# More sets of gathered expert rows multiplied beside the dense half of a PEER layer

## The chip, the core and the metric

The kernel runs on one core of a Trainium2 chip. Five engines work from queues of their own, each in order: TensorE (PE in the profile, PEld its weight loads), VectorE (DVE), ScalarE (ACT), GpSimd (POOL) and SyncE (SP). Data comes by DMA, issued from the queues of SP, ACT and POOL; indirect gathers are issued from POOL. TensorE writes to PSUM, which has eight banks of 128 x 512 floats. The metric is the device time of one execution in microseconds.

## What is computed

One layer of a diffusion backbone on 256 latent tokens and 256 context tokens, width 2048: a modulated norm, an input projection, a bidirectional mLSTM and differential attention, their merge, an output projection, and then the part that matters here, a PEER retrieval over 16384 single-neuron experts, and a final norm. The PEER part in the reference:

```python
def peer(h, w_pq, sub_keys, expert_u, expert_v):
    q = (h @ w_pq).reshape(B, T, P_HEADS, 2, P_KEY_DIM // 2)          # 8 heads
    s = jnp.einsum('bthpd,hpnd->bthpn', q, sub_keys)                  # 2 x 128 keys
    s1, i1 = lax.top_k(s[..., 0, :], P_TOPK)                          # 16 of each
    s2, i2 = lax.top_k(s[..., 1, :], P_TOPK)
    cand_s = (s1[..., :, None] + s2[..., None, :]).reshape(...)
    cand_i = (i1[..., :, None] * N_KEYS + i2[..., None, :]).reshape(...)
    top_s, pos = lax.top_k(cand_s, P_TOPK)
    idx = jnp.take_along_axis(cand_i, pos, axis=-1)
    g = jax.nn.softmax(top_s, axis=-1)
    def block(args):                                                  # 128 tokens
        act = jax.nn.gelu(jnp.einsum('td,ted->te', hx, expert_u[ix]))
        return jnp.einsum('te,ted->td', gx * act, expert_v[ix])
```

Each token uses 8 x 16 experts: it needs the dot product of its vector with the expert's row of `expert_u`, a gelu, the gate, and the sum of the experts' rows of `expert_v` with these weights.

## The kernel before

Matrices are split into a part rounded to TensorE's fast float form ("hi") and the rest ("lo"): ACT casts, DVE (in one of four cases POOL) subtracts (`stage`, lines 126 to 137), and three products are summed.

**U.** All 16384 rows of `expert_u` are multiplied with all tokens, whether they are used or not. The experts form 128 columns of 128. `u_pair` (1219) takes two columns: for each, 32 products, 16 with "hi" against both parts of the tokens (128x512) and 16 with "lo" (128x256), into one bank of the pool `psS`, which has four. The loop at 1631 then reduces the bank with DVE (1640), applies the gelu on ACT (1641) and writes the activations to a table in DRAM, `ag_dram`, from ACT's queue (1645). `made[0]` counts the columns so far.

Beside U, in small steps, runs a generator, `plan` (1463): after every half column `pump(pace[0])` (253) takes some steps of it, `pace[0]` of them on average (1.7 while the lists are made, then 1.25 and at last 1.3). It does the two top-16 searches (`retrieve`), writes the gates into the same DRAM table (`gate_map`, `map_out`), and makes lists of the used experts (`lists`, 1299). When 126 columns are through, `drain()` (1633) runs what is left of it at once.

**Blocks.** The 256 tokens are two tiles of 128, each of four groups of 32. A used expert goes into a block of 128 experts of one kind. Kinds 0 to 3 hold experts that only one group of tile 0 uses, kinds 4 to 7 the same for tile 1, six blocks each (`CAPS`, 57); other kinds are for experts of one tile, of one group in each tile, and of any tokens. `fill` (1347) gives places in the order of the columns: the first five blocks of each group from the columns under `EARLY` = 104, the sixth from all 126 (loop at 1391). The last two columns are taken whole. Four blocks, one of each group of a tile, are a set: `SETS[t][i]`.

**V.** For a block, POOL gathers 128 rows of `expert_v`, 8 KB each (`stage_rows`, 1507), and the experts' activations and gates from `ag_dram` (`stage_gates`, 1519; for the first five blocks only from the columns under `EARLY`). DVE multiplies these into weights (`weights_of`, 1542). In a set each block fills only 32 of TensorE's columns, and `v_groups` (1592) issues the four groups side by side, 16 products (32 instructions in the trace) for the 2048 output columns. The sum of a tile stays in four PSUM banks, `out_acc[t]`. Those of tile 0 are there as soon as `psG`, two banks of the lists, is released at the start of `soon` (1600); those of tile 1 take the place of `psS` when U is over (1654).

`soon` is the last part of `plan`. It gathers the rows of the first two sets, waits until `EARLY` columns are made, and then takes set after set: gates and rows of one set while the set before is multiplied. Its list is `SOON`, five sets of tile 0, which are multiplied beside U, and the first two of `ITEMS`, which are only gathered. After U the rest of `ITEMS` follows: two whole columns, a mixture of sets, paired, shared and single blocks, and at the end three sets. Before the last two sets the sum of tile 0 is closed, and its residual, norm and output run beside them.

**What sets the order.** Products go to TensorE, gathers to POOL and U's loads to SP in program order (`keep_in_program_order`). Everything else is placed by a planner in the build that simulates a timeline. Rows lie in a ring: four buffers of two rows until U is over, six after that (`two_rows`, 1494).

Of the kernel before, what the change touches and what calls it, by code (L numbers as in the profile page):

```python
# [19 lines left out]
F32 = mybir.dt.float32  # L20
# [6 lines left out]
OP = mybir.AluOpType  # L27
AX = mybir.AxisListType
PSUM = bass.MemoryType.PSUM
DRAM = bass.MemoryType.DRAM  # L30

P = 128
D = 2048
T = 256
# [18 lines left out]


N_LIST = P - 2
EARLY = 104
CAPS = (6,) * 8 + (8, 8, 16) + (1,) * 16
BASE = tuple(sum(CAPS[:i]) for i in range(len(CAPS)))
BOTH, PAIR, DENSE = 10, 11, 27
TILES = [(g // 4,) for g in range(8)] + [(0,), (1,)] + [(0, 1)] * 17  # L60
# [12 lines left out]
def spread(*groups):  # L73
    return [x for _, _, x in sorted(((i + 0.5) / len(g), j, x) for j, g in enumerate(groups) for i, x in enumerate(g))]
# [2 lines left out]


SETS = [[[(4 * t + j, i) for j in range(4)] for i in range(6)] for t in range(2)]
SOON = SETS[0][:5]  # L80
PAIRS = [[(PAIR + 4 * d + g, 0) for g in range(4)] for d in range(4)]
ITEMS = SETS[1][:2] + [[(DENSE, i)] for i in range(N_LIST, P)] + spread(
    SETS[1][2:4], PAIRS, [[(BOTH, i)] for i in range(CAPS[BOTH])], [[(8 + n % 2, n // 2)] for n in range(16)]) + [
    SETS[0][5], SETS[1][4], SETS[1][5]]


def build(tc, a, dump=None):
    nc = tc.nc
# [3 lines left out]
    def mp_(*args, **kw):  # L92
        tc.keep_in_program_order(mm(*args, **kw))  # L93
# [147 lines left out]
    side = []  # L241
# [920 lines left out]
    psM.release()  # L1162
    psA.release()

    psS = tc.alloc_tile_pool(name="psS", bufs=4, space=PSUM, side="right", reuse_waits="tile")
    psG = tc.alloc_tile_pool(name="psG", bufs=2, space=PSUM, reuse_waits="tile")


# [50 lines left out]
    def u_pair(i1, pace):  # L1219
        pss = []  # L1220
        for e in range(2):
            ps = psS.tile([P, 2, T], F32, name="s", tag="s")
            flat = ps.rearrange("p s t -> p (s t)")
            for hf_ in range(2):
                hl = take()
                for kk in range(8):
                    k = hf_ * 8 + kk
                    mp_(flat, lhsT=hl[0][:, kk * P:(kk + 1) * P], rhs=h2hl[k], start=k == 0, stop=False,
                        skip_group_check=True)
                for kk in range(8):  # L1230
                    k = hf_ * 8 + kk
                    mp_(ps[:, 1], lhsT=hl[1][:, kk * P:(kk + 1) * P], rhs=h2[0][k], start=False, stop=k == 15,
                        skip_group_check=True)
                pump(pace[0])
            pss.append(ps)
        return pss
# [62 lines left out]
    def lists():  # L1299
# [88 lines left out]
            nc.vector.tensor_tensor(k3[:, 0], k3[:, 0], gone, op=OP.subtract)  # L1388
        for t in range(2):
            four = single[:, 4 * t:4 * t + 4]  # L1390
            for first, n, w in ((0, CAPS[0] - 1, EARLY), (CAPS[0] - 1, 1, N_LIST)):
                yield from fill(four[:, :, 0:w], n, [BASE[4 * t + c] + first for c in range(4)])
                nc.vector.tensor_tensor(k2[:, t, 0:w], k2[:, t, 0:w], gone[:, 0:w], op=OP.subtract)
                if not first:
                    nc.vector.tensor_tensor(four[:, :, 0:w], four[:, :, 0:w], put[:, :, 0:w], op=OP.subtract)
        nc.vector.tensor_tensor(k3[:, 0], k3[:, 0], k2[:, 0], op=OP.add)
        nc.vector.tensor_tensor(k3[:, 0], k3[:, 0], k2[:, 1], op=OP.add)
# [109 lines left out]
    def stage_rows(kind, i):  # L1507
        raw = one_row()
        if kind == DENSE:
            nc.sync.dma_start(raw, FULL[i * P:(i + 1) * P, :])  # L1510
        else:
            gather(raw, FULL, idxV, BASE[kind] + i)
        return raw

    def gather(out, src, idx, b):
        tc.keep_in_program_order(nc.gpsimd.indirect_dma_start(  # L1516
            out=out, out_offset=None, in_=src, in_offset=bass.IndirectOffsetOnAxis(ap=idx[:, b:b + 1], axis=0)))

    def stage_gates(kind, i):
        if kind == DENSE:  # L1520
            return i
        n = len(TILES[kind])
        ag = gates.tile([P, 4 * P], F32, name="ag", tag="ag", bufs=12)[:, 0:2 * n * P]
        src = (ag_tile, ag_dram)[n - 1]
        gather(ag, src[0:2 * P * (1 + EARLY)] if kind < 8 and i < CAPS[kind] - 1 else src, idxG, BASE[kind] + i)
        return {t: ag[:, 2 * j * P:2 * (j + 1) * P] for j, t in enumerate(TILES[kind])}

    def split(raw):
# [13 lines left out]
    def weights_of(kind, ins):  # L1542
        if kind == DENSE:
            r = halves(act_tail[:, ins - N_LIST, :], T, "d", 2)
            return {t: [x[:, t * P:(t + 1) * P] for x in r] for t in range(2)}
        out = {}
        for t, ag in ins.items():
            if kind < 8 or kind >= PAIR:
                g = slice(32 * group(kind, t), 32 * group(kind, t) + 32)
                out[t] = vst.tile([P, 32], F32, name="w32", tag="w32", bufs=16)  # L1550
                nc.vector.tensor_tensor(out[t], ag[:, g], ag[:, P:][:, g], op=OP.mult)  # L1551
                continue
            w = vst.tile([P, P], F32, name="w", tag="w", bufs=2)
            nc.vector.tensor_tensor(w, ag[:, 0:P], ag[:, P:2 * P], op=OP.mult)
            out[t] = halves(w, P, "l", 5)
        return out
# [31 lines left out]
    made = [0]  # L1588
    out_acc = [None, None]


    def v_groups(t, item, parts, cs=range(4), first=False, last=False):
        for c in cs:
            for (kind, _), (raw, ins) in zip(item, parts):
                q = 32 * group(kind, t)
                mp_(out_acc[t][c][q:q + 32, :], lhsT=ins[t], rhs=raw[:, c * 512:(c + 1) * 512],
                    start=first, stop=last, skip_group_check=True)


    def soon():  # L1600
        nonlocal psG
        psG.release()
        out_acc[0] = accumulators(0)
        work = SOON + ITEMS[:2]
        for n, item in enumerate(work):
            new = []
            if n == 0:
                rows = []
                for b in work[0] + work[1]:
                    rows.append(stage_rows(*b))  # L1610
                    yield
                while made[0] < EARLY:
                    yield
            for j, b in enumerate(item):
                ins = stage_gates(*b)
                yield
                new.append((stage_rows(*b) if n > 1 else rows.pop(0), ins))
                if j == 1 and 0 < n <= len(SOON):
                    parts = [(raw, weights_of(kind, ins)) for (kind, _), (raw, ins) in zip(work[n - 1], held)]
                yield  # L1620
            if 0 < n <= len(SOON):
                v_groups(0, work[n - 1], parts, first=n == 1)
                yield
            held = new
            if n >= len(SOON):
                fetched.extend(new)
                staged[0] += len(new)
# [24 lines left out]


    out_acc[1] = accumulators(1)

    def v_part(hl, ins, t, hf_):
        for sa, sb in PASS:
# [15 lines left out]
        else:  # L1673
            v_block(*parts[0])

    v_groups(1, ITEMS[0], parts, first=True)
    N_FIRST = 4
    for n in range(1, N_FIRST):
        v_item(n)
# [149 lines left out]
```

## Time and profile before

| | us |
|---|---|
| median of 3 runs | 2283.95 (2273.8 to 2288.54) |
| the profiled execution | 2272.16 |
| its span | 2270.4 |
| first reduction of a column of U | at 1175.4 |
| last product of U | 2025.2 |
| last product of V | 2255.7 |
| PE, PEld busy | 95%, 82% of the span |
| DVE, ACT, POOL busy | 67%, 45%, 37% |
| DMA moved | 566.77 MB, 250 GB/s on average |

In the profile a line such as `1977.25 3.64 PE L93 MATMUL v<-vraw,w 128*32 128x512 f32 x32` is a run of instructions: its start and length in us, engine, line of the kernel, operation, the tile written and the tiles read, the shape, the count; in brackets stands an idle time before it and what ended it. L93 is the helper `mp_` through which nearly all products go, so here products are told apart by tiles: `s` is U, `v` is the output sum, `g` are the gate maps and lists. `vraw` are gathered rows, `ag` gathered activations and gates, `w` their product, `raw`, `hi` and `lo` the rows of U and their two parts.

### The profile page before, as it was taken

How to read it: one execution, taken by the hardware profiler on the slowest of the kernel's cores; microseconds unless marked ns; L12 is line 12 of the kernel's file. 1: busy time of each engine (PE TensorE's matmuls, PEld its weight loads, DVE VectorE, ACT ScalarE, POOL GpSimd, SP SyncE). 2: the span in 40 equal slices, each digit the busy share in tenths (PEclk: the TensorE clock that was granted, in tenths of full speed). 3: DMA queues.
4: the chain of work that ended last, by engine and by line, in shares of the span. 5: the costliest groups of instructions: out<-in, count | busy, mean ns of one | idle time of the engine just before them, and what ended most of it. 6: DMA issues, size and time to landing. Idle time of an engine off the chain costs nothing. (4 is left out here: it accounts for less than half of the span.)

```text
span 2270.4 us, 37003 instructions
## 1 busy us (share of the span) xinstructions
PE 2156.6 (95%) x14088; PEld 1865.9 (82%) x14088; DVE 1520.4 (67%) x2739; ACT 1021.6 (45%) x1629; POOL 838.9 (37%) x822
## 2 busy tenths in 40 slices
PE   6999999999999999998998999999999899999994
PEld 3668988999899999986997889987888787766661
DVE  3338793676986777856689867776998444345653
ACT  3232232224565844444444768863455343334441
POOL 2122210235473311000223658852122315556763
PEclk9999999999999999998999999999999999999997
DMA  9958872877555478774555558897655868899997
GB/s 381 368 175 302 319 284 90 299 242 203 165 153 177 140 280 278 267 258 164 185 180 191 175 165 235 229 240 220 202 189 185 329 210 282 327 372 412 413 412 287
DMA packets 235172, 566.77 MB, mean 250 GB/s; under 512 B 85058, under 2 KB 118643, under 8 KB 220912
## 3 DMA queue, kind: packets, MB, share of 16 engines
q1 hardware_dynamic: 153888, 339.34, 44.9%
q0 software_dynamic: 46256, 207.47, 25.0%
q10 hardware_dynamic: 34848, 17.57, 2.7%
q8 instruction: 111, 1.82, 0.3%
q14 instruction: 69, 0.57, 0.1%
HBM read 520.14 MB, written 38.93 MB: 246 GB/s over the span
## 5 line engine op out<-in xcount | busy, mean ns | idle before, releaser
L133 ACT CAST hi<-raw 128x1024 fp32r<-128x1024 f32 x528 | 552.4, 1049 | 817.7 <-PE acc L292 280.4
L136 DVE TENSOR_TENSOR lo<-raw,hi 128x1024 fp32r<-128x1024 f32 x457 | 579.8, 1272 | 338.5 <-ACT hi L133 300.4
L93 PE MATMUL s<-h,hi 128*128 128x512 f32 x2048 | 529.7, 401 | 18.4 <-ACT hi L133 18.4
L93 PEld LDWEIGHTS s<-h,hi 128*128 128x128 f32 x2048 | 371.6, 191 | 92.9 <-ACT hi L133 21.0
L136 POOL TENSOR_TENSOR lo<-raw,hi 128x1024 fp32r<-128x1024 f32 x71 | 181.2, 2552 | 423.2 <-ACT hi L133 394.8
L292 PE MATMUL acc<-hL,hi 128*128 128x256 f32 x2048 | 334.1, 285 | 0.0
L93 PEld LDWEIGHTS s<-h,lo 128*128 128x128 f32 x2048 | 280.9, 192 | 26.8 <-DVE lo L136 3.9
L292 PEld LDWEIGHTS acc<-hL,hi 128*128 128x128 f32 x2048 | 293.3, 192 | 1.8 <-ACT kA L669 0.3
L93 PE MATMUL s<-h,lo 128*128 128x256 f32 x2048 | 288.4, 284 | 2.8 <-DVE lo L136 1.8
L292 PE MATMUL acc<-hL,lo 128*128 128x256 f32 x1024 | 177.0, 286 | 0.7 <-DVE lo L136 0.7
L117 POOL DMA_DIRECT2D raw<-w_mod x128 | 67.9, 531 | 290.4 <-DVE raw L525 277.0
L525 DVE SCALAR_TENSOR_TENSOR raw<-raw,cr 128x1024 f32<-128x1024 f32 x128 | 156.2, 1236 | 21.3 <-DMA raw<-w_mod 17.7
L1253 POOL TENSOR_SCALAR o<-iota,i1T,gT 128x128 f32<-128x128 f32 x128 | 148.0, 1165 | 54.3 <-PE g L93 31.4
L292 PEld LDWEIGHTS acc<-hL,lo 128*128 128x128 f32 x1024 | 151.3, 193 | 2.1 <-DVE lo L136 0.9
L1640 DVE TENSOR_REDUCE act<-s 128x256 f32<-128x512 f32 x126 | 86.4, 686 | 71.0 <-PE s L93 65.0
L1516 POOL DMA_INDIRECT vraw<-expert_v,idxV x96 | 104.6, 1090 | 74.7 <-issue 18.5
L1532 DVE TENSOR_TENSOR lo<-vraw,hi 128x1024 fp32r<-128x1024 f32 x68 | 82.6, 1224 | 65.9 <-ACT hi L1530 65.6
L292 PE MATMUL acc<-hC,hi 128*128 128x256 f32 x512 | 124.7, 283 | 0.0
L1516 POOL DMA_INDIRECT ag<-ag_dram,idxG x96 | 106.2, 1106 | 38.8 <-issue 24.2
L1530 ACT CAST hi<-vraw 128x1024 fp32r<-128x1024 f32 x68 | 70.9, 1049 | 79.6 <-PE v L93 66.4
L93 PE MATMUL v<-hi,l 128*128 128x512 f32 x384 | 105.8, 397 | 0.1
L93 PE MATMUL v<-vraw,w 128*32 128x512 f32 x640 | 81.0, 632 | 20.9 <-DVE w L1551 13.1
(432 smaller groups left out, 3355.9 us busy)
## 6 DMA issues: line engine op xcount, KB each, us to landing
raw<-expert_u SPq DMA_DIRECT2D x256, 512.0 KB, 3.9
raw<-w_in SPq DMA_DIRECT2D x176, 512.0 KB, 4.7
raw<-w_mod POOLq DMA_DIRECT2D x128, 512.0 KB, 5.5
raw<-w_mod SPq DMA_DIRECT2D x64, 512.0 KB, 8.3
raw<-w_out SPq DMA_DIRECT2D x32, 512.0 KB, 3.4
raw<-w_pq SPq DMA_DIRECT2D x32, 512.0 KB, 3.6
ag_dram<-gates SPq DMA_DIRECT2D x32, 512.0 KB, 6.0
ag_dram<-act ACTq DMA_DIRECT2D x126, 128.0 KB, 4.2
```

Source lines behind the costliest of these rows:

```text
L93: tc.keep_in_program_order(mm(*args, **kw))
L117: d = queue.dma_start(r, src)
L133: nc.scalar.copy(h, r)
L136: (nc.vector if shared[0] else nc.gpsimd).tensor_tensor(l, r, h.bitcast(F32), op=OP.subtract)
L292: mm(acc[c][:, g * T:(g + 1) * T], lhsT=hl[sb][:, k2 * 512 + c * P:k2 * 512 + (c + 1) * P], rhs=rhs(sa, g, k), start=first and k2 == 0 and ...
L525: product = nc.vector.scalar_tensor_tensor(r, r, 1.0, cr, op0=OP.mult, op1=OP.mult, accum_out=part[:, h, i:i + 1])
L1253: (nc.gpsimd if i % 2 else nc.vector).tensor_scalar(o2[:, i], iota, cols[:, i:i + 1], factor[:, i:i + 1], op0=OP.is_equal, op1=OP.mult)
L1516: tc.keep_in_program_order(nc.gpsimd.indirect_dma_start(out=out, out_offset=None, in_=src, in_offset=bass.IndirectOffsetOnAxis(ap=idx[:, b ...
L1530: nc.scalar.copy(h, raw)
L1532: nc.vector.tensor_tensor(l, raw, h.bitcast(F32), op=OP.subtract)
L1640: nc.vector.reduce_sum(act[:, e], ps.rearrange("p s t -> p t s"), axis=AX.X)
```

## The change

Seven sets instead of five are multiplied beside U, of the two tiles in turn: `SETS[0][0]`, `SETS[1][0]`, `SETS[0][1]`, ... `SETS[0][3]`. `SETS[1][3]` and `SETS[0][4]` are gathered beside U and multiplied right after it. So nine sets are gathered in `soon` instead of seven, and the mixture in V loses two sets.

- Columns. The first four blocks of each group come from the columns under 86, so the gathers can begin there. Of tile 0, the fifth comes from the columns under 108 and the sixth from all; of tile 1, the fifth and sixth from all. Tile 0 has three fills in the lists where it had two.
- Steps. The products of a set are issued in four parts of eight instructions (`multiply`), one part per step, between the gathers of the next set, instead of all at once.
- Tile 1's sum. While U runs there are no four banks for it. Each part goes into one bank `vs`, taken from U's ring, which has three banks now. The first set's parts are copied from there to SBUF by ACT (`kept`), the other two sets' parts are added to that by DVE. After U, four products with the identity matrix put the kept sums into the banks of tile 1, where the later sets are added.

```diff
-EARLY = 104
+EARLY, LATER = 86, 108
+GOES = {0: ((4, EARLY), (1, LATER), (1, N_LIST)), 4: ((4, EARLY), (2, N_LIST))}
-SOON = SETS[0][:5]
+SOON = [SETS[i % 2][i // 2] for i in range(7)]
-ITEMS = SETS[1][:2] + [[(DENSE, i)] for i in range(N_LIST, P)] + spread(
-    SETS[1][2:4], PAIRS, [[(BOTH, i)] for i in range(CAPS[BOTH])], [[(8 + n % 2, n // 2)] for n in range(16)]) + [
+ITEMS = [SETS[1][3], SETS[0][4]] + [[(DENSE, i)] for i in range(N_LIST, P)] + spread(
+    PAIRS, [[(BOTH, i)] for i in range(CAPS[BOTH])], [[(8 + n % 2, n // 2)] for n in range(16)]) + [
     SETS[0][5], SETS[1][4], SETS[1][5]]
...
-    psS = tc.alloc_tile_pool(name="psS", bufs=4, space=PSUM, side="right", reuse_waits="tile")
+    psS = tc.alloc_tile_pool(name="psS", bufs=1, space=PSUM, side="right", reuse_waits="tile")
...
-            ps = psS.tile([P, 2, T], F32, name="s", tag="s")
+            ps = psS.tile([P, 2, T], F32, name="s", tag="s", bufs=3)
...
-            for first, n, w in ((0, CAPS[0] - 1, EARLY), (CAPS[0] - 1, 1, N_LIST)):
+            first = 0
+            for n, w in GOES[4 * t]:
                 yield from fill(four[:, :, 0:w], n, [BASE[4 * t + c] + first for c in range(4)])
                 nc.vector.tensor_tensor(k2[:, t, 0:w], k2[:, t, 0:w], gone[:, 0:w], op=OP.subtract)
-                if not first:
+                first += n
+                if w < N_LIST:
                     nc.vector.tensor_tensor(four[:, :, 0:w], four[:, :, 0:w], put[:, :, 0:w], op=OP.subtract)
...
-        gather(ag, src[0:2 * P * (1 + EARLY)] if kind < 8 and i < CAPS[kind] - 1 else src, idxG, BASE[kind] + i)
+        gather(ag, src[0:2 * P * (1 + columns_of(kind, i))] if kind < 8 else src, idxG, BASE[kind] + i)
...
+    def multiply(n, item, parts):
+        t = n % 2
+        for c in range(4):
+            if t == 0:
+                v_groups(0, item, parts, (c,), first=n == 0)
+            else:
+                ps = psS.tile([P, 512], F32, name="vs", tag="vs", bufs=1)
+                v_groups(1, item, parts, (c,), first=True, last=True, into=ps)
+                if n == 1:
+                    kept.append(gm.tile([P, 4, P], F32, name="kept", tag=("o1", "o2")[c // 2], bufs=3).rearrange(
+                        "p a b -> p (a b)"))
+                    nc.scalar.copy(kept[c], ps)
+                else:
+                    nc.vector.tensor_tensor(kept[c], ps, kept[c], op=OP.add)
+            yield
...
         work = SOON + ITEMS[:2]
+        rows = []
+        for b in work[0] + work[1]:
+            rows.append(stage_rows(*b))
+            yield
+        held, going = None, iter(())
         for n, item in enumerate(work):
             new = []
-            if n == 0:
-                rows = []
-                for b in work[0] + work[1]:
-                    rows.append(stage_rows(*b))
+            for j, b in enumerate(item):
+                while made[0] < columns_of(*b):
                     yield
-                while made[0] < EARLY:
-                    yield
-            for j, b in enumerate(item):
                 ins = stage_gates(*b)
                 yield
-                new.append((stage_rows(*b) if n > 1 else rows.pop(0), ins))
+                next(going, None)
+                new.append((rows.pop(0) if rows else stage_rows(*b), ins))
                 if j == 1 and 0 < n <= len(SOON):
-                    parts = [(raw, weights_of(kind, ins)) for (kind, _), (raw, ins) in zip(work[n - 1], held)]
+                    going = multiply(n - 1, work[n - 1], [
+                        (raw, weights_of(kind, ins)) for (kind, _), (raw, ins) in zip(work[n - 1], held)])
                 yield
-            if 0 < n <= len(SOON):
-                v_groups(0, work[n - 1], parts, first=n == 1)
+                next(going, None)
+            for _ in going:
                 yield
...
     out_acc[1] = accumulators(1)
+    for c in range(4):
+        mp_(out_acc[1][c], lhsT=ident, rhs=kept[c], start=True, stop=False, skip_group_check=True)
...
-    v_groups(1, ITEMS[0], parts, first=True)
+    v_groups(1, ITEMS[0], parts)
```

More of the change, by code (lines that the diff above doesn't have):

```diff
@@ L1517, in gather, with columns_of @@
             out=out, out_offset=None, in_=src, in_offset=bass.IndirectOffsetOnAxis(ap=idx[:, b:b + 1], axis=0)))
+    def columns_of(kind, i):
+        for n, w in GOES[kind // 4 * 4]:
+            if i < n:
+                return w
+            i -= n
     def stage_gates(kind, i):
@@ L1589, in build, with v_groups @@
     out_acc = [None, None]
-    def v_groups(t, item, parts, cs=range(4), first=False, last=False):
+    def v_groups(t, item, parts, cs=range(4), first=False, last=False, into=None):
         for c in cs:
@@ L1595, in v_groups @@
                 q = 32 * group(kind, t)
-                mp_(out_acc[t][c][q:q + 32, :], lhsT=ins[t], rhs=raw[:, c * 512:(c + 1) * 512],
+                mp_((into or out_acc[t][c])[q:q + 32, :], lhsT=ins[t], rhs=raw[:, c * 512:(c + 1) * 512],
                     start=first, stop=last, skip_group_check=True)
+    kept = []
+    def multiply(n, item, parts):
[13 more added lines that the diff above has]
+            yield
     def soon():
```

## The prediction

> **What bounds the kernel now.** I read the busy table by stage first, then how many columns of U end in each stage, then the order of TensorE's work around U's end, and last the queues. The profiled execution took 2272.16 us, 2270.4 of them span and 1.8 around it. In the stage rows the columns after the two times are its length, then busy time (and instructions) of PE, weight loads, DVE, ACT and POOL, the clock, the DMA share and GB/s.
>
> ```profile
> 1753.80:1808.20 54.40, 46.46 (x259) 39.60 (x258) 26.20 (x39) 19.60 (x21) 19.22 (x12) 1.00 0.85 319
> 1808.20:1864.00 55.80, 55.80 (x321) 49.11 (x320) 24.83 (x25) 24.48 (x26) 11.98 (x5) 1.00 0.69 219
> 1864.00:2026.00 162.00, 157.50 (x937) 124.73 (x938) 69.70 (x87) 54.12 (x59) 84.25 (x61) 0.98 0.84 310
> 2025.20:2040.00 14.80, 12.06 (x74) 4.35 (x75) 6.90 (x12) 4.75 (x8) 9.70 (x10) 0.88 1.01 416
> 2040.00:2220.00 180.00, 179.85 (x935) 124.40 (x933) 102.73 (x200) 78.55 (x111) 123.64 (x115) 1.00 1.02 413
> 2220.00:2254.00 34.00, 15.80 (x88) 4.62 (x91) 12.46 (x23) 3.39 (x9) 16.90 (x16) 0.75 0.91 369
> ```
>
> U ends at 2025.2, and V begins. In V's long middle TensorE is busy 179.85 of 180 us and the DMA engines move 413 GB/s at a share of 1.02: two limits at once. Only in V's last 34 us does TensorE wait. Beside U the DMA engines are below that rate. The next rows are the same three stretches of U for the reduction of a column (line 1640) alone: its count is the number of columns.
>
> ```profile
> 1753.80:1808.20 54.40, 5.50 (x9) 1.00 0.85 319
> 1808.20:1864.00 55.80, 6.91 (x10) 1.00 0.69 219
> 1864.00:2026.00 162.00, 17.18 (x25) 0.98 0.84 310
> ```
>
> Ten columns in 55.8 us are 5.58 us a column, with TensorE never idle. The first stretch begins and ends on a reduction, so its nine hold 8 columns: 44.6 us of work in 54.4, 9.8 us lost while eight row gathers arrive at once. The third's 25 begin with one at its very start: 24 columns, 133.9 us, and five sets.
>
> ```profile
> 1976.21 1.11 PE L93 MATMUL s<-h,lo 128*128 128x256 f32 x8
> 1977.25 3.64 PE L93 MATMUL v<-vraw,w 128*32 128x512 f32 x32
> 1980.82 2.14 PE L93 MATMUL s<-h,hi 128*128 128x512 f32 x8
> 1982.80 1.10 PE L93 MATMUL s<-h,lo 128*128 128x256 f32 x8
> 1983.73 2.00 PE L93 MATMUL s<-h,hi 128*128 128x512 f32 x8
> 2024.09 1.11 PE L93 MATMUL s<-h,lo 128*128 128x256 f32 x8
> 2151.52 7.07 PE L93 MATMUL v<-vraw,w 128*32 128x512 f32 x64
> 2175.52 3.64 PE L93 MATMUL v<-vraw,w 128*32 128x512 f32 x32
> ```
>
> From the start of "lo" to the next "hi" is 4.61 us with a set between and 0.93 without, so a set costs U 3.68 us. Two sets in one stretch take 3.43 more than one (7.07 against 3.64): 3.43 is the work and 0.25 the price of entering and leaving a stretch of 32-column matmuls. Five sets are 18.4 us; with the columns 152.3 of some 161, so 9 us are lost in the third stretch, and 19 in U after the lists.
>
> **The change part by part, in U.** Sets go from five to seven, and each is cut into four stretches: 28 x (0.86 + 0.25) = 31.1 us where 18.4 stood, +12.7. U is TensorE's own time, so nothing hides this unless it falls into a wait. 5.8 us of the 12.7 are the extra 23 stretch prices.
>
> [...] If a switch were free the term would be 24.1 - 18.4, some +6 instead of +13.
>
> Three of the seven sets are of tile 1 and go through one PSUM bank: 12 evacuations, four by ACT, eight by an add on DVE. The nearest row is an add from PSUM of this very size, and beside it stand the waits that queue with it:
>
> ```profile
> L1716 DVE TENSOR_TENSOR yf<-v,vraw 128x512 f32<-128x512 f32 x4 | 2.8, 690 | 2.5 <-PE v L93 2.5
> DVE w L1551 <- DMA ag<-ag_dram,idxG: 39.3, 19, 4.8
> DVE lo L136 <- ACT hi L133: 111.6, 66, 4.3
> POOL ag L1516 <- DMA ag_dram<-act: 11.4, 2, 11.1
> L136 DVE TENSOR_TENSOR lo<-raw,hi 128x1024 fp32r<-128x1024 f32 x48 | 58.4, 1218 | 5.9 <-ACT hi L133 5.8
> ```
>
> A chunk of 0.86 us must wait until the last one's 0.69 us add is done. The pump makes 1.3 steps per half column (2.8 us), so mostly a half column lies between two chunks and hides the add; about four times in twelve nothing does, some 1 us each. Bounds: 0, and 12 x (0.69 + 1.22), an add behind one "lo", 23 us. I take +4, nearer to the lower, as DVE is busy only 69.7 of 162 us here. Queued behind a waiting add are the next "lo" (TensorE's next weights) and the column reductions; queued ahead may be one of the "w" products, which wait for gate gathers 39.3 us in 19 waits; there will be 28 of these in U where there were 20.
>
> Two moves cost nothing here. U's ring of PSUM banks goes from four to three; a bank is wanted again two columns later, 11.2 us, and the longest lag of a reduction that I found is this one:
>
> ```profile
> 1466.92 1.12 PE L93 MATMUL s<-h,lo 128*128 128x256 f32 x8
> 1475.86 0.68 DVE L1640 TENSOR_REDUCE act<-s 128x256 f32<-128x512 f32 x1
> ```
>
> done 8.5 us after the column's end at 1468.0; were the cover gone, every microsecond of lag over 11.2 would stop TensorE. And POOL's 11.1 us wait at column 104 for the activations just written goes, as the gathers ask for columns under 86 only; its queue held a "lo" then, worth under 1 us to TensorE.
>
> The lists get a fifth fill of single-group blocks: two more matmuls and some ten small DVE operations.
>
> ```profile
> L93 PE MATMUL g<-single,from_on 128*128 128x416 bf16 x2 | 0.7, 349 | 0.0
> 1756.90 1.06 POOL L1516 DMA_INDIRECT vraw<-expert_v,idxV  x1 [6.64 <-DVE idxV L1456]
> 1872.22 0.96 POOL L1516 DMA_INDIRECT ag<-ag_dram,idxG  x1 [11.12 <-DMA ag_dram<-act]
> 2239.55 0.94 POOL L1516 DMA_INDIRECT vraw<-expert_v,idxV  x1 [0.30 <-issue]
> ```
>
> 2 x 0.35, +1 us. The indices are ready at 1756.9, at column 85; the fill's six steps at 1.7 a pump put that two columns later, the eight row gathers three more, so gates start near column 91 instead of 104. 72 steps at 5.2 per pair of columns are 28 columns: done by 119 or so, with seven to spare before the drain at 126. Worked out on the reference's inputs, the new caps leave no expert over, like the old, so the fallback loop stays empty.
>
> Those eight blocks more beside U are DMA. What a block weighs, and what the queues carry now, in V (2026 to 2246) and in late U (1870 to 2026):
>
> ```profile
> DMA packets 14951, 90.90 MB, mean 413 GB/s; under 512 B 2266, under 2 KB 2266, under 8 KB 5462
> vraw<-expert_v,idxV POOLq DMA_INDIRECT x68, 11.6
> ag<-ag_dram,idxG POOLq DMA_INDIRECT x67, 10.9
> DMA packets 16179, 48.94 MB, mean 314 GB/s; under 512 B 1778, under 2 KB 7434, under 8 KB 13699
> ```
>
> A block is 128 rows of 8 KB and 128 gate rows of 1 KB, 1.18 MB; eight are 9.4 MB. From 1753.8 to 2026 the three stage rows give 79.8 MB; 89.2 in some 290 us would be 308 GB/s, no more than late U has now, and the quiet stretch of 219 fills up. Bounds: -9 (spreading ends the late loss) and +12 (bursts saturate more often); I take +3, the 9 us per five sets continued to seven. U together: 12.7 + 4 + 1 + 3, +21.
>
> **In V.** Two sets fewer in the middle: -7.1. Both first sets lie ready at U's end, so the first wait below (2.74) goes: -2.7. New are four full-width products of the identity with the kept sums. No row shows one; four 32-column matmuls run side by side in 0.86 us, and a full one cannot take less, so 3.4 at least; wider weights and a stretch price add up to 2; I take +4.
>
> ```profile
> 2032.36 5.29 PE L93 MATMUL v<-vraw,w 128*32 128x512 f32 x26 [2.74 <-DMA vraw<-expert_v,idxV]
> 2220.08 1.05 PE L93 MATMUL v<-vraw,w 128*32 128x512 f32 x4
> 2222.46 1.02 PE L93 MATMUL v<-vraw,w 128*32 128x512 f32 x2 [1.33 <-DMA vraw<-expert_v,idxV]
> 2227.22 5.17 PE L93 MATMUL v<-vraw,w 128*32 128x512 f32 x28 [3.74 <-DMA vraw<-expert_v,idxV]
> 2241.15 4.20 DVE vraw L1734
> 2245.51 10.16 PE L93 MATMUL v<-vraw,w 128*32 128x512 f32 x62 [13.13 <-DVE w L1551]
> ```
>
> At the end the third-last set spreads over 2220.1 to 2232.4 because its rows come late. 9.4 MB less at 413 GB/s put the DMA engines 22.8 us ahead, so it takes 3.6 us: -8.7. Then the gain stops: the last set's rows go into buffers that this set frees, POOL issues eight gathers at 1.25 us, its last at 2239.55, and only then the tile-0 ending (the 4.20 us DVE row) and the last weights follow. That tail of 23 us stays but for faster landings, -2. V together: -16.5, not 22.8: the middle becomes TensorE's.
>
> The sum is +4.5 us on 2272.16, 2276.7 for the profiled execution. The runs' median, 2283.95, lies 11.8 above it; I carry the difference over: 2288.
>
> **The rivals.** *Faster, chance 0.17.* U's 19 us of waits swallow the new chunks, and the DMA engines catch up while TensorE multiplies; V returns all of the 22.8 and a bit of the tail. For it: the waits exist. Against it: most come in one burst before any set is multiplied. U +2, V -25: 2261.
>
> *Slower, chance 0.15.* The single bank decides. DVE and ACT work in order, the "w" products wait up to 4.8 us for gates, "lo" up to 4.3 for ACT; if an evacuation sits behind such a wait TensorE stands at the next chunk. At 2.5 us on average this is 30 instead of 4: 2314. It costs over 1% from some 1.9 us on each. Against it: DVE is more than half idle there.
>
> [...]
>
> *The gathers crowd U's own loads, chance 0.15.* Late U already reaches bursts at the ceiling; the sets lose +14 rather than +3: 2299.
>
> *It does not do what it says, chance 0.05.* Lists end so late that the last sets fall to the drain: U's cost stays, V gains some 5: 2300.
>
> **How the numbers follow.** My forecast, 2288, has the remaining 0.48. 1% is 22.8 us, about what can be told from no change. Faster by that is half of the first rival, 0.08. Slower by that: most of the second (0.11), parts of the third and fourth (0.05), a little of the forecast (0.02), 0.18. The rest, 0.74, is no change. The range, 2266 to 2310, takes in the crowding case, the late one and the bounds of the wait terms nearly whole, and leaves out the outer halves of the first two rivals.
>
> **What would show it.** From column 85 on, U at 7.0 us a column, sets included, in place of 6.5 (272 us over 42); U's end near 2046; first gate gather near 1800; the 13 us wait before the last sets still there, those at 2222 and 2227 gone; DMA in V's middle under 413 GB/s with TensorE still full. I am wrong if evacuations stop TensorE for over 2 us each, if U's end moves by less than 10 us, or if V shortens by the whole 22.8.

## The result and the profile after

The changed kernel takes 2298.14 us (median of 19, 2290.03 to 2307.81) beside 2283.17 of the kernel before (median of 19, 2273.8 to 2295.02): a ratio of 1.0065, 95% interval 1.0048 to 1.0082, some 15 us slower. That is inside the range of the forecast and inside "within 1%", but 10 us above the point when measured from the medians, and the sign is sure. On another chip, on which most experiments ran, it was 1.0028, 1.0009 to 1.0046. Two executions, one of the changed kernel and one of a variant of it, took 9178 and 11247 us and are in no ratio here.

The profiled execution after took 2307.81 us, span 2306.1: 35.7 more than the profiled one before. This pair overstates the change: the profiled execution before, at 2272.16, was faster than all 19 timed ones, and the one after is the slowest of its 19. Three stretches account for the 35.7: TensorE began U 7.6 us later, ahead of anything the change touches, and needed 2.9 less for the columns 0 to 85, where of the change only the three banks of U's ring act; U from column 85 took 33.5 more; V (U's last product to V's last) 2.5 less; and what follows is the same 14.7.

First U from the end of column 85, before and then after: in each case the row of the stage (length; busy time and count of PE, weight loads, DVE, ACT, POOL; clock; DMA share; GB/s), and behind it TensorE's groups in the same stretch (busy, mean ns of one | idle before them and what ended it).

```profile
1753.80:2025.20 271.40, 258.96 (x1510) 213.33 (x1512) 120.04 (x149) 98.16 (x103) 114.92 (x77) 0.99 0.81 293
```

```profile
L93 PE MATMUL s<-h,hi 128*128 128x512 f32 x672 | 171.3, 397 | 11.3 <-ACT hi L133 11.3
L93 PE MATMUL s<-h,lo 128*128 128x256 f32 x672 | 94.8, 284 | 1.1 <-POOL lo L136 0.8 <-DVE lo L136 0.2
L93 PE MATMUL v<-vraw,w 128*32 128x512 f32 x164 | 18.8, 596 | 0.0
```

```profile
1758.50:2063.40 304.90, 279.35 (x1586) 218.84 (x1585) 125.83 (x174) 100.21 (x110) 132.44 (x93) 0.97 0.81 298
```

```profile
L94 PE MATMUL s<-h,hi 128*128 128x512 f32 x672 | 176.1, 405 | 14.3 <-ACT hi L134 14.3
L94 PE MATMUL s<-h,lo 128*128 128x256 f32 x673 | 96.0, 286 | 5.2 <-DVE lo L137 4.4 <-POOL lo L137 0.8
L94 PE MATMUL v<-vraw,w 128*32 128x512 f32 x128 | 18.3, 609 | 4.1 <-DMA vraw<-expert_v,idxV 4.1
L94 PE MATMUL vs<-vraw,w 128*32 128x512 f32 x96 | 12.8, 605 | 2.0 <-DVE kept L1623 1.2 <-ACT kept L1621 0.8
```

TensorE is busy 20.4 us longer and idle 13.1 longer. Busy: the sets 31.1 where 18.8 stood, +12.3; U's own products, the same count, +6.0, since each takes longer (405 ns for 397, the clock 0.97 for 0.99); most of the rest is 1.9 of the lists' products, which now reach past column 85. Idle: +4.2 on DVE's "lo", +4.1 on gathered rows, +3.0 on ACT's "hi", +2.0 on the evacuations of the single bank.

Now V, from U's end to V's end, before and after: TensorE's groups, and the row of the stage.

```profile
L93 PE MATMUL v<-hi,l 128*128 128x512 f32 x384 | 105.8, 397 | 0.1
L93 PE MATMUL v<-vraw,w 128*32 128x512 f32 x480 | 62.8, 644 | 20.9 <-DVE w L1551 13.1 <-DMA vraw<-expert_v,idxV 7.8
```

```profile
2025.30:2256.00 230.70, 209.28 (x1104) 133.60 (x1096) 123.98 (x238) 87.50 (x131) 150.85 (x141) 0.96 0.99 403
```

```profile
L94 PE MATMUL v<-hi,l 128*128 128x512 f32 x384 | 106.7, 400 | 13.9 <-PEq L1717 13.9
L94 PE MATMUL v<-vraw,w 128*32 128x512 f32 x416 | 49.9, 616 | 13.0 <-DVE w L1560 13.0
L94 PE MATMUL v<-kept,ident 128*128 128x512 f32 x8 | 3.6, 592 | 0.0
```

```profile
2063.50:2291.50 228.00, 201.00 (x1048) 133.38 (x1046) 120.88 (x224) 87.03 (x128) 133.60 (x125) 0.94 0.91 358
```

The single-group products fall by 12.9 us and all 7.8 us of waits for rows are gone; the kept sums cost 3.6. TensorE's busy time is 8.3 less. But a wait of 13.9 us that was nowhere before stands in front of a "hi" product, put down to TensorE's own sequencer at line 1717: the branch over the fallback loop. From there V runs in one piece to the wait of 13 us before the last sets, as the chain of waits after shows, where before it went through ACT, DVE, POOL and gathers. Of each chain a part, before and then after:

```profile
2049.19 120.34 PE v L93 x630
...
2203.57 18.76 DMA vraw<-expert_v,idxV
...
2223.09 12.59 DMA vraw<-expert_v,idxV
```

```profile
2099.16 168.42 PE v L94 x864
...
2276.35 0.62 POOL rf L203
2276.97 0.03 issue
2277.00 4.21 DVE vraw L1764
2281.20 0.11 DVE w L1560
```

### The profile page after: what moved, and what is told of

Read it like the earlier page. It is cut to its first block, busy times and chain, and to the rows that moved or that the text cites. A ratio compares the mean times of both kernels' runs of the same rounds, so it can differ in the third digit from the quotient of the medians.

```text
span 2306.1 us, 37028 instructions
## 1 busy us (share of the span) xinstructions
PE 2171.4 (94%) x14098; PEld 1873.4 (81%) x14098; DVE 1525.6 (66%) x2762; ACT 1025.1 (44%) x1633; POOL 833.3 (36%) x822
## 5 line engine op out<-in xcount | busy, mean ns | idle before, releaser
L137 POOL TENSOR_TENSOR lo<-raw,hi 128x1024 fp32r<-128x1024 f32 x71 | 175.7, 2475 | 445.7 <-ACT hi L134 366.8
L526 DVE SCALAR_TENSOR_TENSOR raw<-raw,cr 128x1024 f32<-128x1024 f32 x128 | 156.2, 1235 | 24.3 <-DMA raw<-w_mod 18.8
L94 PE MATMUL v<-hi,l 128*128 128x512 f32 x384 | 106.7, 400 | 13.9 <-PEq L1717 13.9
L94 PEld LDWEIGHTS v<-hi,l 128*128 128x128 f32 x384 | 72.6, 190 | 34.8 <-issue 17.7
```

What stands on the lines that cost most here:

```text
L137: (nc.vector if shared[0] else nc.gpsimd).tensor_tensor(l, r, h.bitcast(F32), op=OP.subtract)
L526: product = nc.vector.scalar_tensor_tensor(r, r, 1.0, cr, op0=OP.mult, op1=OP.mult, accum_out=part[:, h, i:i + 1])
```

## The experiments

The profiles of all runs are read by the same two figures: U from the end of column 85 to its last product, and V. The first eleven runs went to two further chips, the last to a third; a ratio is always to the kernel before on the same chip.

| kernel | ratio (95%) | U from column 85 | V |
|---|---|---|---|
| before, first profile | 1 | 271.4 | 230.5 |
| before, second profile | 1 | 275.3 | 260.9 |
| after, first profile | 1.0065 (1.0048 to 1.0082) | 304.9 | 228.0 |
| after, second profile | | 300.6 | 229.1 |
| after, third profile | 1.0028 (1.0009 to 1.0046) | 304.8 | 222.5 |
| after, no fallback | 0.9993 (0.9971 to 1.0016) | 304.5 | 224.5 |
| before, no fallback | 0.9977 (0.9948 to 1.0007) | 274.0 | 251.6 |
| before, sets cut in four | 1.0059 (1.0025 to 1.0094) | 281.0 | 241.7 |
| before, early columns | 1.0021 (0.9987 to 1.0056) | 280.3 | 239.2 |
| before, three sets beside U | 1.0004 (0.9980 to 1.0029) | 265.4 | 255.6 |
| before, branch later | 1.0001 (0.9975 to 1.0027) | 273.1 | 246.8 |
| after, tile 0's sets whole | 1.0010 (0.9982 to 1.0039) | 296.7 | 228.8 |
| after, branch later | 1.0009 (0.9982 to 1.0037) | 303.3 | 229.3 |
| after, both edits | 0.9985 (0.9964 to 1.0007) | 298.5 | 229.4 |

**Is the branch's wait the kernel's, or an accident?** The changed kernel again, without an edit:

> The changed kernel, unaltered, a second look. In the first look TensorE stood 13.9 us at the branch of the fallback (line 1717), and U from column 85 on took 33.5 us more than before. Theory A (the branch wait belongs to the kernel): 10 to 15 us again, time 2290 to 2308. Theory B (an accident of that execution, which was at the slow end of its runs): under 3 us at the branch, time under 2297.

Then both kernels without the branch and the loop behind it, which handles experts left over by the lists; there are none on these inputs.

```diff
-        rest = nc.values_load(n_over[0:1, 0:1], min_val=0, max_val=N_EXPERTS)
-    with tc.If(rest > 0):
-        with tc.For_i(0, N_LIST, 1) as i:
-            ...
```

> The changed kernel without the fallback for experts that fit no list (read of the count, branch and loop left out; the lists leave none over on these inputs, so nothing else of the result changes). Theory A: the wait at the branch is all that goes, 10 to 14 us less than the changed kernel: 2284 to 2288, a ratio near 1.001. Theory B: within 3 us of the changed kernel, ratio 1.005 to 1.007.

> The kernel before, without the fallback (left out as in the last one). There TensorE lost 0.6 us at the branch. Both theories: 0 to 3 us less than before, ratio 0.998 to 1.0. Should it gain 10 us or more, the branch costs both kernels and does not explain the difference.

The second profile of the changed kernel showed the wait again, and without the branch it was gone. The rows of line 1717 on TensorE's sequencer, of the changed kernel, and those of the same line (1687) of the kernel before:

```profile
L1717 PEldq COMPARE_BRANCH  x1: 228/228/228, 2081.5 to 2081.5; - x1
L1717 PEldq EVENT_SEMAPHORE  x1: 51/51/51, 2099.1 to 2099.1; - x1
```

```profile
L1687 PEldq COMPARE_BRANCH  x1: 231/231/231, 2045.3 to 2045.3; - x1
L1687 PEldq EVENT_SEMAPHORE  x1: 51/51/51, 2049.1 to 2049.1; - x1
```

From the branch to TensorE's next event it is 17.6 us in one and 3.8 in the other. So far it looked like a property of the kernel: without the branch the changed kernel is even with the kernel before (0.9993). But V was only 3.5 to 4.6 us shorter than in the two profiles with the wait, not 14: several waits of 1 to 3 us on "issue" stood there instead. The kernel before gained nothing that can be told from its noise (0.9977).

**What cutting a set costs by itself.** The kernel before, its five sets in four parts each, one part per step:

```diff
+        def quarters(item, parts, first):
+            for c in range(4):
+                v_groups(0, item, parts, (c,), first=first)
+                yield
...
-            if 0 < n <= len(SOON):
-                v_groups(0, work[n - 1], parts, first=n == 1)
+            for _ in going:
```

> The kernel before with each of its five sets beside U issued in four parts, one per step, as the change does. Price per stretch theory (1.2 us for a part of eight in the changed kernel, 3.7 for a whole set): 5 x (4.8 - 3.7) = +5.5 us, less where two parts follow each other, ratio 1.002. Rival, parts fall into waits that are there anyway or give the row gathers air: 0 or a gain, ratio under 1.0005.

The sets' products in U, which are 18.8 us whole, became this in the same count:

```profile
L93 PE MATMUL v<-vraw,w 128*32 128x512 f32 x164 | 22.4, 603 | 1.6 <-DMA vraw<-expert_v,idxV 1.6
```

That is +3.6 of busy time for at most 15 more stretches, so at least 0.24 each, beside the 0.25 of the prediction. U as a whole was 6 to 10 us longer than in the two profiles of the kernel before. The time rose by 0.59%, 13 us, which is more than U shows and above both expectations. The profile is of an execution of 2292.11 us, one of the two fastest of the ten, whose median is 2307.89; so where the usual execution loses the rest is not shown.

**The changed kernel with fewer cuts, the earlier start alone, the branch elsewhere, and the kernel before again.** The four edits, in this order:

```diff
-        for c in range(4):
-            if t == 0:
-                v_groups(0, item, parts, (c,), first=n == 0)
+        if t == 0:
+            v_groups(0, item, parts, first=n == 0)
+            yield
+        for c in range(4 * t):
...
```

```diff
-EARLY = 104
+EARLY, LATER = 86, 108
+GOES = {0: ((4, EARLY), (1, LATER), (1, N_LIST)), 4: ((4, EARLY), (2, N_LIST))}
...
+                while made[0] < columns_of(*b):
+                    yield
```

```diff
-    N_FIRST = 4
+    N_FIRST = 16
```

> The changed kernel, but the four sets of tile 0 that are multiplied beside U are issued whole, 32 instructions in one step, as before; the three of tile 1 stay in four parts. Twelve of the 28 stretches of 32-column products go. Theory A (a stretch has a fixed price, as the traces show it: a single part of eight adds 1.20 us to its column where its share of a whole set is 0.92): TensorE saves 12 x 0.28 = 3.4 us, U from column 85 takes 297 to 301 us in place of 300.6 and 304.9, and the ratio to the kernel before is about 1.005 in place of 1.0065. Theory B (cutting costs by far more, since the five cut sets of the other run cost 13.6 us in the time, 2.7 us a set): four whole sets give back 11 us, the ratio is 1.0017. Rival C (short stretches are what lets waits be hidden; a whole set holds up 'lo' and the reductions): U gets no shorter and the ratio is 1.0065 or more.

> The kernel before with the change's columns alone: the first four blocks of each group from the columns under 86, the fifth of tile 0 under 108, and each gather waits for its own columns. Still five sets of tile 0, each whole, four banks for U, nothing kept. Theory A: the earlier start costs the two matmuls and some ten small operations of the fifth fill, +1 us, and spreads the gathers; U from column 85 takes 268 to 275 us where it took 271.4, the ratio is 0.998 to 1.002. Rival (gathers that begin at column 91 instead of 104 crowd U's own loads, whatever their number): TensorE's gaps in U after column 85 rise from 16.0 to 24 or more, as in the changed kernel (28.0 and 24.8), U takes 280 or more, the ratio is 1.004 or above.

> The changed kernel with the branch of the fallback loop twelve items later in V (after item 15 in place of item 3). [...] Theory B (it is the load of the DMA queues by then: V of the changed kernel has them at a share of 1.01 throughout its middle): the wait is 10 to 18 us again at the new place and the ratio stays at 1.005 to 1.008. Theory C (the wait is hidden work that V would lose elsewhere): the wait goes but the ratio stays.

> The kernel before, unchanged, for a second profile of it on this chip. Theory A (the branch's wait belongs to a kernel): TensorE's branch and its next semaphore event lie 3 to 5 us apart, as the 3.8 us of the first profile, and V takes 228 to 235 us. Rival (V of the first profile was a fortunate one): waits of 2 to 7 us on issue or on the gathered rows lie in V's middle, and V takes 240 us or more, as in the two profiles with one part changed (241.7 and 251.6).

*Whole sets.* U fell to 296.7, 4 to 8 us, and the tile-0 products to 14.6 us in the stretch (18.3 cut): the sets' busy time falls from 31.1 to 27.4 for at most 12 stretches, 0.31 each. The ratio, 1.0010, is not told apart from 1.0028 of the changed kernel on that chip.

*The earlier start alone* cost U 5 to 9 us where +1 was expected. TensorE's idle time is 15.4 us against 12.4 and 14.7 in the two profiles of the kernel before. Its two groups of U:

```profile
L94 PE MATMUL s<-h,hi 128*128 128x512 f32 x672 | 175.5, 404 | 9.4 <-ACT hi L134 9.3
L94 PE MATMUL s<-h,lo 128*128 128x256 f32 x672 | 95.9, 286 | 6.0 <-DVE lo L137 4.2 <-POOL lo L137 1.8
```

The waits on "hi", which ACT casts from the loaded rows, fell (9.4 where the two profiles have 11.3 and 13.4), and those on "lo" rose (6.0 where they have 1.1 and 1.3), so it is not U's loads that were crowded. The timed ratio fits both theories. The trace names what it is. The same thing is in the changed kernel; here are DVE's and TensorE's rows in order of time, and then three short stretches by stage, whose last three columns are clock, DMA share and GB/s.

```profile
1811.32 0.19 DVE L1560 TENSOR_TENSOR w<-ag 128x32 f32<-128x32 f32 x1 [4.68 <-DMA ag<-ag_dram,idxG]
1811.43 1.23 DVE L137 TENSOR_TENSOR lo<-raw,hi 128x1024 fp32r<-128x1024 f32 x1
```

```profile
1806.58 2.11 PE L94 MATMUL s<-h,hi 128*128 128x512 f32 x8 [0.67 <-ACT hi L134]
1812.71 2.08 PE L94 MATMUL s<-h,lo 128*128 128x256 f32 x8 [4.02 <-DVE lo L137]
1814.58 3.61 PE L94 MATMUL s<-h,hi 128*128 128x512 f32 x8
1818.00 1.49 PE L94 MATMUL s<-h,lo 128*128 128x256 f32 x8
1819.32 1.99 PE L94 MATMUL s<-h,hi 128*128 128x512 f32 x8
```

```profile
1800.00:1808.00 8.00, 7.33 (x40) 6.18 (x40) 2.61 (x3) 2.63 (x3) 4.41 (x3) 1.00 1.01 417
1814.00:1818.00 4.00, 4.00 (x13) 3.23 (x13) 0.95 (x1) 1.04 (x1) 3.54 (x3) 0.50 0.84 258
1820.00:1824.00 4.00, 4.00 (x23) 3.45 (x22) 2.33 (x3) 1.68 (x2) 0.34 (x1) 1.00 0.94 286
```

The first gate product "w" waits 4.68 us in DVE's queue for its gather, which shares full DMA engines (417 GB/s) with row gathers and U's loads. The "lo" of a column of U is queued behind it, and TensorE stands 4.02 us. Then it runs at half clock, 0.50 granted, for some 6 us: eight "hi" products take 3.61 us instead of 2.11, the "lo" on either side 2.08 and 1.49 instead of 1.11, 2.9 us more. Together 7 us for one gather, in this profile. All eight profiles with the early columns have this wait, 2.2 to 4.6 us; no profile of the kernel before with the old columns has one on "lo" that costs more than 1.4 us in all.

*The branch later.* TensorE's 14 us at the branch were gone, 3.8 us lay between branch and next event and other work hid them. V was no shorter, though: a wait of 11.28 us for "hi" stood in V's middle instead. Theory C by the trace; the ratio, 1.0009, decides nothing.

*The kernel before again* gave the other half of the answer. It has 3.8 us from the branch to the next event, as the first profile has, but V took 260.9 us in place of 230.5. The group that answers to the one above:

```profile
L93 PE MATMUL v<-hi,l 128*128 128x512 f32 x384 | 109.9, 409 | 16.3 <-ACT hi L1530 14.0 <-issue 2.2
```

The first profile of before, on which the whole sum rested, was of an execution without these waits; the second is from another chip. In the six profiles with the kernel before's V (those of the table except that with three sets) it takes 230.5 to 260.9 us, 245 on average; in the seven with the changed V 222.5 to 229.4, 227 on average.

**The changed kernel on the same chip, both edits together, and the exchange alone.** The last takes two sets out of U:

```diff
-SOON = SETS[0][:5]
+SOON = SETS[0][:3]
-    SETS[1][2:4], PAIRS, [[(BOTH, i)] for i in range(CAPS[BOTH])], ...
+    [SETS[0][3], SETS[1][2], SETS[0][4], SETS[1][3]], PAIRS, [[(BOTH, i)] for i in range(CAPS[BOTH])], ...
```

> The changed kernel, unchanged, timed beside the kernel before on the chip on which the variants ran, since the ratio 1.0065 comes from another chip. Theory A (the change costs what the traces show: U from column 85 +28 to +30 us, V -16 against a usual V of the kernel before of some 245 us): +12 to +15 us, ratio 1.005 to 1.007, and the variants at 1.0009 and 1.001 are real gains of 0.4 to 0.6 %. Rival (on this chip the two kernels stand otherwise; the one look at the changed kernel here, 2293.5, was no slower than the kernel before): ratio 0.998 to 1.002, and the variants gained nothing.

> The changed kernel with both edits: tile 0's four sets issued whole, and the fallback's branch after item 15. If both are gains and lie in different stages they add up: 6 us in U and up to 10 in V, ratio 0.996 to 0.999, and U from column 85 takes 296 to 298 us. If what was gained by moving the branch is lost again in V's middle (V took 229.3 us with the branch moved and 228.8 with the cuts taken away, the same), the ratio is 1.000 to 1.003, and V is at 228 to 230 again with a wait of some 11 us on gathered rows.

> The kernel before with three whole sets of tile 0 beside U in place of five; the fourth and fifth go into V's mixture. It prices the exchange itself, in the other direction and without the cutting, the bank or the lists. Theory A, as in the prediction (V's middle is TensorE's as soon as the DMA engines have some room, and in the usual run of the kernel before it has waits on rows): U from column 85 is 7.4 us shorter, some 264 to 268; V gets the two sets' 7.1 us of products and more waits, by 9.4 MB at 413 GB/s up to 22.8 us; with the -16.5 of the prediction turned round the sum is +9, ratio 1.004. Rival (TensorE alone bounds V, so the exchange is even): ratio 0.999 to 1.001. Rival (the DMA engines alone bound it): U -7.4, V +22.8, +15 us, ratio 1.0067.

The changed kernel is slower on this chip too, by 0.28%, less than on the first; theory A's 1.005 to 1.007 lies outside the interval, and only the interval's lower end lies in the rival's 0.998 to 1.002. Its third profile has the branch's wait at 5.8 us:

```profile
2085.57 2.05 PE L94 MATMUL v<-hi,l 128*128 128x512 f32 x4 [5.79 <-PEq L1717]
```

and the kernel before with three sets has it at 8.08 us, where the kernel before itself had none. So the theory A of the first runs falls: the length of the wait belongs neither to the kernel nor to the branch's place alone.

*What ends the wait at the branch.* The traces also keep the time of every raise of a semaphore (the counter by which one engine tells another that it is done), though no view prints them. The event of TensorE behind the branch waits for a semaphore that TensorE's own products raise when they end, and in all twelve profiles with the branch it comes 0.03 us after the last raise. In the first profile of the changed kernel the last eight raises belong to products that ended between 2076.4 and 2085.3, but they came in pairs at 2077.7, 2083.4, 2089.8 and 2099.0. TensorE had been done: the trace has no product of it between 2085.3 and 2099.2, and its granted clock is 0.50 from 2088.5 on, as it is behind the wait of 4.02 us in U. ACT, which overwrites what these products read, waits for the same raises and starts right behind them; the view calls them "remote":

```profile
2089.91 1.04 ACT L1539 CAST hi<-vraw 128x1024 fp32r<-128x1024 f32 x1 [5.36 <-remote]
2099.00 1.04 ACT L1539 CAST hi<-vraw 128x1024 fp32r<-128x1024 f32 x1 [8.04 <-remote]
```

So the 13.9 us are not the price of a branch. They are late raises, and the branch makes TensorE itself wait for them. With the branch moved, DVE stood 13.3 us on such a raise and ACT 8.1 and 5.4, and TensorE's 11.28 us for "hi" followed from that. The spread of V goes with them: in the first profile of the kernel before no raise in V came more than 0.1 us after the end of a product that raises it; in each of the other thirteen 25 to 62 of some 150 did. Why they come late is not shown.

With both edits the ratio is 0.9985, its interval just clear of the changed kernel's: the two gains add up to 0.4%. It is not told apart from the kernel before. U was 298.5 us, just over the 296 to 298 that were expected; V, at 229.4, was not shorter, with a wait of 5.2 us on "issue" and 3.2 on "hi" early in it.

Taking two sets from U cost nothing, ratio 1.0004: U fell by 6 to 10 us, 7.4 expected, and V, at 255.6, is 10.5 above the average of 245. V's single-group products in this kernel:

```profile
L93 PE MATMUL v<-vraw,w 128*32 128x512 f32 x544 | 69.9, 611 | 17.5 <-DVE w L1551 14.1 <-issue 3.1
```

64 more take 7.1 us more than the 62.8 of the first profile. A set is worth the same on either side: the rival on TensorE was right, the two with DMA were not.

**The kernel before with the branch later.**

> The kernel before with the fallback's branch after item 15 of V, the edit that the changed kernel had in two runs. Theory A (the branch costs the changed kernel 6 to 14 us but the kernel before at most its own 3.8 us between branch and next event, which other work hides): nothing to gain, ratio 0.998 to 1.002, so that the changed kernel with both edits, at 0.9985, is even with the best form of the kernel before. Rival (the branch's wait falls on either kernel by chance, as the 5.8 us of the last profile of the changed kernel and the 8.1 us of the kernel before with three sets suggest; moved, it costs neither): ratio 0.994 to 0.998, as much as the changed kernel gained, and U from column 85 stays at 271 to 276 us with V at 225 to 240.

Nothing gained, 1.0001, with V at 246.8: the forecast of theory A, though not for its reason, since the wait does not belong to the branch. What both edits gained is thus not to be had in the kernel before by moving the branch.

## Why the prediction was right, and where not

*The sets, +12.7.* Measured 12.3 in busy time. The 3.68 of a set, the 0.86 of a part and the 0.25 of a stretch all held; the cut and the whole sets give at least 0.24 and 0.31 for the last. The prediction's +6 for a free switch leaves the switches of the five whole sets in the 18.4; without them it is two sets of 3.43, +6.9.

*The evacuations, +4, and the rival of the single bank.* 2.0 us in all for the waits on "kept", 0.17 for each of the twelve, not the 2 us that the rival needs nor the 0.69 of a whole add. DVE's queue did hold up TensorE, as the rival argued, but through "lo" and not through the bank.

*The DMA stalls beside U, +3 between -9 and +12.* Here the sum failed. The waits on "hi", "lo" and rows rose by 11.3 us, near the upper bound, and U's own products by 6.0 through the clock (0.97 for 0.99), for which there was no term at all. One cause is shown: the first "w" waits for a gate gather with "lo" behind it, some 7 us here (a wait of 2.2 to 4.6 us in all eight profiles with the early columns). The prediction had named "lo" as queued behind "w", but put no term for it into the sum; in the trace of before the longest such wait, 4.8 us, happened to be covered. The 4.1 us for rows are in four of the seven profiles (2.3 to 4.5) of the changed kernel and its variants; what brings them was not tested. U rose by 33.5 instead of 21, by 30 in the mean of the unedited profiles, and ended at 2063 instead of 2046.

*Lists, +1.* 1.9 us of their products lie past column 85.

*V, -16.5.* By its parts: the products of sets -12.9 (-7.1 forecast for the two sets; the rest probably the third-last set, no longer in pieces), waits for rows -7.8 (first wait and third-last), the kept sums +3.6 (+4), the other products +1.4 by the clock (0.94 for 0.96). That is -15.7: right. V's middle did become TensorE's, with 364 GB/s in place of 413:

```profile
2110.00:2220.00 110.00, 110.00 (x573) 76.92 (x572) 65.99 (x126) 50.55 (x75) 69.61 (x65) 1.00 0.92 364
```

The two waits at 2222 and 2227 are gone, that of 13 us before the last sets stayed. But this profile then lost 13.9 us at the branch, and V ended only 2.5 earlier. Late raises of TensorE's semaphore were in no part of the sum: V in the trace of before has none, and 3.8 us at the branch. Over all profiles V falls from 245 to 227 on average, by 18, since V of the kernel before usually has waits of its own that its first profile lacked.

*Carrying the 11.8 us between the profiled execution and the median over* was a step that hid this. V of the kernel before varies by 30 us between its two profiles and that of the changed one by 7 among its three, so the difference is no constant. That the point was only 10 us low is in part luck, since errors cancel: U was 9 to 12 us dearer; the -16.5 was taken off a V of 230.5 us, against which the average V of the changed kernel, 227, is only 3 less; and the 11.8 us carried over, about what the usual V of the kernel before has above its first profile (245 against 230.5), made up for most of those 13 lost. With U +30 and V -18 the sum is +12 on the medians; measured were +15 on the first chip and +6 on the other (0.28%).

*The rivals.* The faster one is refuted: U's waits swallowed nothing, they grew. The crowding one came nearest in size (2299), but its cause was not U's loads: in the early start alone the waits on "hi" fell, while one gate gather stopped DVE's queue and with it "lo". That the change does not do what it says is refuted by the order in the trace: vs products in all their 96 instructions lie in U.

*What stays open.* Why TensorE's semaphore is raised up to 14.1 us late in one execution and on time in another; every "remote" wait of more than 5 us on ACT and DVE in V is for it. And how the 15 and 6 us of the medians divide: the cuts, the copies and the gather are priced in the traces, but no single edit of the changed kernel is told apart from it in time, and cutting alone cost the kernel before 13 us, of which its trace shows less.

## What to carry to other kernels

Moving work beside a stage that is itself TensorE's is an exchange at par at best: here a set costs 3.7 us where it goes and 3.6 where it leaves, and every cut, copy and earlier gather comes on top. Before an operation that waits for a DMA is moved earlier, look what stands behind it in its engine's in-order queue, and count with a TensorE wait the half clock that can follow it: here it did behind six of eight waits of 3.5 to 4.6 us. One profile is one execution: where two profiles of the same kernel differ by 30 us in a stage, a term of that stage must be read from several. A wait that the profile puts down to a branch or calls "remote" is to be followed to the semaphore that ended it before the branch is blamed.

## What was not expected of the hardware

- TensorE's semaphore was raised long after the product that raises it had ended: in the first profile of the changed kernel by up to 13.8 us, with the DMA engines full (share 1.01), and not at all in V of the first profile of the kernel before, which had them as full (1.02). So from the compare of the branch to TensorE's next event it took 17.6, 17.9 and 9.0 us in three profiles of one program, and 3.8 in two of the other. The view of the DMA queues shows one packet of an instruction queue some 2 us behind the branch, after 2083.5, but TensorE went on only at 2099.1, right behind the last raise, so this trace does not show a wait for that packet.
- In U, in the first profiles of the two kernels, the granted clock is 0.50 for 3.4 or 6.8 us behind six of the eight waits of 3.5 to 4.6 us, which at that clock costs 1.7 or 3.4 us. Not always: at 1784.88 in the first profile of the kernel before a wait of 3.52 us had no slow product behind it.

The first of these rows of TensorE's order is of the kernel before, the second of the changed one:

```profile
1784.88 2.11 PE L93 MATMUL s<-h,hi 128*128 128x512 f32 x8 [3.52 <-ACT hi L133]
```

```profile
1787.24 3.07 PE L94 MATMUL s<-h,hi 128*128 128x512 f32 x8 [3.71 <-ACT hi L134]
```
